# One decoder layer on one core: the first block of x on another queue, a shorter run-up, the first weight cast split over two engines, and one output block of the last 128 tokens in two pieces

## The chip, the cores and the metric

The kernel runs on one core of a Trainium2 chip. The core has TensorE (matmul, written PE in the profile, its weight loads PEld), VectorE (DVE), ScalarE (ACT), GpSimd (POOL) and SyncE (SP); SP and ACT each issue DMAs into a queue of their own (SPq, ACTq). The metric is the device time of one execution in microseconds (us), the median of several runs.

## What is computed

One layer over 256 tokens of width 2048, all in float32:

```
h = rmsnorm(x, norm_mix_w);  proj = h @ w_in          # w_in: 2048 x 16416
q, k, v (conv + silu) -> gated delta rule over 16 heads -> rmsnorm * silu(z)
p_in -> causal means over 2, 4, 8, 16 tokens -> pool_w
x = x + (sigmoid(g_a) * y_a + sigmoid(g_b) * y_b) @ w_out
h = rmsnorm(x, norm_ffn_w);  gate, up = h @ w_up      # 2048 x 11264
x = x + (gelu(conv(gate) + b) * up) @ w_down          # 5632 x 2048
y = rmsnorm(x, norm_final_w)
```

The weights are read once, about 300 MB, and every product is made of three: each float32 operand is split into a high part, rounded to the float32r type in which TensorE multiplies, and a low part, the remainder; high x high, low x high and high x low are summed.

## The kernel before, in words

**Weights.** `srcs` lists the weight blocks in the order of their use, mostly 256 rows x 512 columns (0.5 MB). `load` (L120) has SP read the next block into one of four `raw` buffers; the first two blocks (`HALVES = 2`) are read in two halves of 128 rows each. `begin` (L136) splits a block: ScalarE casts `raw` to `whi` (L144), then VectorE subtracts to get `wlo` (L152). For the first two blocks `begin_half` (L128) does the same for one half at a time (L133, L134).

**Start.** GpSimd writes a tile of ones, and TensorE multiplies ones by ones (`runup`, L241), nine times before anything else; a float32 matmul appears as two records in the profile. The rows of `norm_mix_w` are read by ScalarE's queue (L255); a copy of one column behind that read (L258) has ScalarE load its table early. SP reads x in column blocks of 512, both groups of 128 tokens at once, the first block in two halves of 256 columns (L263). Its row of issues is: x 0 first half, weight block 0 (two halves), x 0 second half, weight block 1 (two halves), x 1, weight blocks 2 and 3, x 2, x 3.

**First products.** From L319 the order of TensorE, VectorE and ScalarE is the order of the program text. TensorE transposes `nmrows` (L321), VectorE copies that to `nmw`. Then, for each of four groups of 128 rows of w_in: TensorE transposes x (`turn_x`, L281; two groups at a time), ScalarE scales the transposed x to its high part `xhi` (L287), VectorE makes the low part `xlo` (L288), `begin_half` splits the half weight block, and TensorE multiplies (`products_k0`, L313): high x high, low x high, high x low, for two groups of tokens each, so six matmuls. Behind the first split stands a second run-up of four matmuls (L332); the products of a group are issued one group later than its split. From the third weight block on, whole blocks are split by `begin`.

**Middle.** All later projections, the delta rule, the pooling, w_out, w_up and w_down follow; TensorE's work there is not touched by the change. Outside L319 to L351 and one later stretch, a planner orders the instructions by a simulated timeline.

**End.** w_down's last products are ordered so that the four column blocks of the first 128 tokens (t = 0) finish ahead of those of the last 128 (t = 1). For each block VectorE adds the residual (L1142), ScalarE sums the squares (L1145), and for blocks 0 to 2 VectorE multiplies by the final gain (L1147). When all blocks of a t are done, the root is taken (L1149 to L1152, the last on GpSimd), and `scaled` multiplies the blocks by it and writes them out: blocks 2 and 3 on VectorE, 0 and 1 on ScalarE, each 128 x 512 with one DMA of 256 KB (L1128), in the order 2, 0, 3 on SP's queue and 1 on ScalarE's.

Of the kernel before, what the change touches and what calls it, by code (L numbers as in the profile page):

```python
# [7 lines left out]
F32 = mybir.dt.float32  # L8
F32R = mybir.dt.float32r
I32 = mybir.dt.int32  # L10
AF = mybir.ActivationFunctionType
ALU = mybir.AluOpType

P = 128
# [20 lines left out]
def kernel(  # L35
# [20 lines left out]
    nc = tc.nc  # L56
# [11 lines left out]
    def nm(s):  # L68
        cnt[0] += 1
        return f"{s}_{cnt[0]}"  # L70

    def pg(shape=(P, 512)):
        return psg.tile(list(shape), F32, tag="g", name=nm("psg"))
# [35 lines left out]
    loads = []  # L109
# [4 lines left out]
    def weights(ahead=AHEAD):  # L114

        begin(taken[0] + ahead + 1)
        taken[0] += 1
        return made[taken[0] - 1]

    def load(n):  # L120
        while len(loads) < min(len(srcs), n):
            src = srcs[len(loads)]
            raw = wpool.tile(list(src.shape), F32, tag="raw", name=nm("raw"), bufs=4)
            for k in range(2) if len(loads) < HALVES else (slice(None),):
                last_load[0] = nc.sync.dma_start(raw[:, k], src[:, k]).ins
            loads.append(raw)

    def begin_half(n, k):  # L128

        if k == 0:  # L130
            made.append(tuple(wpool.tile([P, 2, 512], F32R, tag=tag, name=nm(tag)) for tag in ("whi", "wlo")))
        hi, lo = made[n]
        nc.scalar.copy(hi[:, k], loads[n][:, k])  # L133
        nc.vector.tensor_tensor(lo[:, k], loads[n][:, k], hi[:, k].bitcast(F32), op=ALU.subtract)  # L134

    def begin(n):  # L136
# [104 lines left out]
    def runup(n):  # L241
        for _ in range(n):
            mm(pr0[:, 0, :P], ones, ones, start=True, stop=True)  # L243


    runup(9)

    def mtile(i, shape, dt, name):
        return big.tile(shape, dt, tag=f"m{i}", name=name)

    mix = tc.tile_pool(name="mix", bufs=1)
    mp = mix.__enter__()

    nmrows = mp.tile([KD, P], F32, tag="w1", name="nmrows")
    rows = nc.scalar.dma_start(nmrows, norm_mix_w[0].rearrange("(r p) -> r p", p=P))  # L255
    first = cpool.tile([P, 1], F32, name="first")
    with tc.issue_after(rows.ins):
        nc.scalar.copy(first, ones[:, 0:1])  # L258
    x0 = []
    for c in range(4):  # L260
        xc = mtile(c, [P, 2, 512], F32, f"x0_{c}")
        for h in ((0, 256), (256, 512)) if c == 0 else ((0, 512),):
            nc.sync.dma_start(xc[:, :, h[0] : h[1]], x[0, :, c * 512 + h[0] : c * 512 + h[1]]  # L263
                              .rearrange("(t p) d -> p t d", p=P))
            if h[0] == 0:
                load(min(c + 1, 4))
        x0.append(xc)
        load(min(2 * c + 2, 4))


    nmw = cpool.tile([P, KD], F32, name="nmw")
# [3 lines left out]
    def turn_x(c, ks=range(4)):  # L275

        pts = []
        for k in (4 * c + k for k in ks):
            pt = pg([P, S])
            for t in range(2):  # L280
                nc.tensor.transpose(pt[:, t * P : (t + 1) * P], x0[c][:, t, (k % 4) * P : (k % 4 + 1) * P], ident)  # L281
            pts.append((k, pt))
        return pts

    def parts_x(pts):
        for k, pt in pts:
            hi = nc.scalar.activation(xhi[:, k, :], pt, AF.Copy, scale=nmw[:, k : k + 1])  # L287
            lo = nc.vector.scalar_tensor_tensor(xlo[:, k, :], pt, nmw[:, k : k + 1], xhi[:, k, :].bitcast(F32),  # L288
                                                op0=ALU.mult, op1=ALU.subtract)
        return hi.ins, lo.ins  # L290
# [17 lines left out]
    def products_k0(c, kks, hi, lo):  # L308
        for w, part in ((hi, xh), (hi, xl), (lo, xh)):
            for kk in kks:  # L310
                k = 2 * c + kk
                for t in range(2):
                    mm(ps_k0[:, t, :], part(k, t), w[:, kk, :], start=(k == 0 and w is hi and part is xh),  # L313
                       stop=(k == KD - 1 and w is lo))

    def tile_k0(c):
        products_k0(c, range(2), *weights(-1))

    with tc.manual_schedule(engines={mybir.EngineType.PE, mybir.EngineType.DVE, mybir.EngineType.Activation}):  # L319
        pt = pg()  # L320
        nc.tensor.transpose(pt[:, :KD], nmrows, ident[:KD, :KD])  # L321
        nc.vector.tensor_copy(nmw, pt[:, :KD])

        n = 0
        for c in range(HALVES):
            for k in range(2):
                if k == 0:
                    pts = turn_x(0, (2 * c, 2 * c + 1))
                parts_x(pts[k : k + 1])
                begin_half(c, k)  # L330
                if n == 0:
                    runup(4)  # L332
                else:
                    products_k0((n - 1) // 2, ((n - 1) % 2,), *made[(n - 1) // 2])
                n += 1
        taken[0] = HALVES
        for c in range(4):
            if c:
                tile_k0(2 * c)
            if c < 3:  # L340
                pts = turn_x(c + 1)
                parts_x(pts[:2])
                begin(2 * c + 3)
                last_act, last_dve = parts_x(pts[2:])
                begin(2 * c + 4)
                square_x(c)
            if c:
                tile_k0(2 * c + 1)
            else:
                products_k0(1, (1,), *made[1])  # L350
        square_x(3)  # L351
# [110 lines left out]
    for c in range(2):  # L462
        hi, lo = weights()
        for kk in range(8):
            k = 8 * c + kk
# [399 lines left out]
    for g in range(4):  # L865
# [70 lines left out]
        def gate(ps, tag):  # L936
            th = mp.tile([P, 2, 512], F32, tag=tag, name=nm("gate"))
            for t in range(2):
# [6 lines left out]
                                       op0=ALU.add, op1=ALU.mult)  # L945
# [69 lines left out]
    xt = fp.tile([P, 2, D], F32, name="xt")  # L1015
    for c in range(4):
        cs = slice(c * 512, (c + 1) * 512)
# [4 lines left out]
    for c in range(4):  # L1022
# [4 lines left out]
        xs = xt[:, :, c * 512 : (c + 1) * 512]  # L1027
# [4 lines left out]
        for k2 in range(2):  # L1032
            pt = pg([P, 2, S])
            for kk in range(2):
                k = 4 * c + 2 * k2 + kk
                for t in range(2):
                    nc.tensor.transpose(pt[:, kk, t * P : (t + 1) * P], xt[:, t, k * P : (k + 1) * P], ident)
            for kk in range(2):
                k = 4 * c + 2 * k2 + kk
# [3 lines left out]
                                               op0=ALU.mult, op1=ALU.subtract)  # L1043
# [36 lines left out]
    nfin = big.tile([P, D], F32, tag="xhl", name="nfin")  # L1080
# [34 lines left out]
    rs = cpool.tile([P, 2], F32, name="rsf")  # L1115
    for t in range(2):
        ts = slice(t, t + 1)

        def scaled(c, by, queue):
            xs = xt[:, t, c * 512 : (c + 1) * 512]  # L1120
            if by is nc.scalar:
                nc.scalar.activation(xs, xs, AF.Copy, scale=rs[:, ts])
            elif c < 3:
                nc.vector.tensor_scalar(xs, xs, rs[:, ts], None, op0=ALU.mult)
            else:
                nc.vector.scalar_tensor_tensor(xs, xs, rs[:, ts], nfin[:, c * 512 : (c + 1) * 512],
                                               op0=ALU.mult, op1=ALU.mult)
            queue.dma_start(out[0, t * P : (t + 1) * P, c * 512 : (c + 1) * 512], xs)  # L1128

        blocks = [(c, slice(0, 512), None) for c in range(4 - t)]
        if t:
            blocks += [(3, slice(0, 256), None), (3, slice(256, 512), acc[0][0])]
        for n, (c, cs, ps) in enumerate(blocks):
            more = {} if ps is None else dict(ps=ps, first=2 * (LAST - 1))
            if c:
                down_part(LAST - 1, c, t, *ws[c], cs, **more)
            down_part(LAST, c, t, *wk[c], cs, **more)
            xs = xt[:, t, c * 512 : (c + 1) * 512]  # L1140
            sums = cs if ps is not None else slice(0, 512)
            nc.vector.scalar_tensor_tensor(xs[:, sums], (acc[c][t] if ps is None else ps)[:, sums], rs2[:, ts],  # L1142
                                           xs[:, sums], op0=ALU.mult, op1=ALU.add)
            jk = cpool.tile([P, 512], F32, tag="sqj", name=nm("sqj"))
            nc.scalar.activation(jk[:, cs], xs[:, cs], AF.Square, accum_out=ssq5[:, t, n : n + 1])  # L1145
            if c < 3:
                nc.vector.tensor_tensor(xs, xs, nfin[:, c * 512 : (c + 1) * 512], op=ALU.mult)  # L1147
        n = len(blocks) - 1
        nc.vector.tensor_reduce(part[:, ts], ssq5[:, t, 0:n], axis=mybir.AxisListType.X, op=ALU.add)  # L1149
        nc.vector.tensor_scalar(part[:, ts], part[:, ts], 1.0 / D, EPS, op0=ALU.mult, op1=ALU.add)  # L1150
        nc.vector.tensor_scalar(rs[:, ts], ssq5[:, t, n : n + 1], 1.0 / D, part[:, ts], op0=ALU.mult, op1=ALU.add)
        nc.gpsimd.tensor_tensor(rs[:, ts], rs[:, ts], epsx[:, 0:1], op=ALU.pow)  # L1152
        scaled(2, nc.vector, nc.sync)
        scaled(0, nc.scalar, nc.sync)
        scaled(3, nc.vector, nc.sync)
        scaled(1, nc.scalar, nc.scalar)

# [30 lines left out]
```

## Time and profile before

| | |
|---|---|
| median of 3 runs | 1562.16 us (1561.58 to 1562.27) |
| profiled execution | 1561.54 us, span 1559.8 us |
| mean granted TensorE clock | 0.998 |
| HBM read, written | 297.56 MB, 5.27 MB (194 GB/s over the span) |
| DMA share in the 40 slices | 0.6 to 0.8 in most, 0.2 in the last |

The span runs from the first to the last instruction. In the views, a line of the timeline gives start, length, engine, line of the code, operation, output<-inputs, shapes, and in square brackets the idle time ahead of it with what ended it; a line of the chain of waits gives start, length and what the chain went through; a line of the windows view gives for each engine its busy time and number of instructions, then granted clock, share of the DMA engines and GB/s.

### The profile page before, as it was taken

To read this page: it belongs to the slowest core of one execution; us is meant where nothing else is said; L and a number is where in the kernel's file an instruction comes from. 1 tells how busy PE (TensorE), PEld (TensorE's weight loads), DVE (VectorE), ACT (ScalarE), POOL (GpSimd) and SP (SyncE) were. 2 spreads that over 40 slices of the span, in tenths; PEclk is the share of its full clock that TensorE was granted. 3 is DMA by queue.
4 is the path that set the end of the run, shared out by engine and by line. 5 is a ranking of instruction groups with operands and counts; after the bars stand their busy time and mean duration, and the time that the engine had idled before them with its cause. 6 is when DMAs were issued, how large, how long until landed. Compare 5 with 4: busy or idle time off the path is not lost.

```text
span 1559.8 us, 21250 instructions
## 1 busy us (share of the span) xinstructions
PE 1551.1 (99%) x7996; PEld 1304.0 (84%) x7996; DVE 1092.2 (70%) x1705; ACT 749.2 (48%) x969; POOL 52.2 (3%) x54
## 2 busy tenths in 40 slices
PE   9999999999999999999999999999999999999998
PEld 8878888888888888888888888888888888888886
DVE  6899758996699858896656666776666667444445
ACT  6545445454555445454544544444444444334443
POOL 1020001000010001000000000000000000000000
PEclk9999999999999999999999999999999999999999
DMA  8677657676676656675666666666666666666662
GB/s 273 201 239 200 186 161 223 204 204 183 174 218 202 194 174 191 211 205 174 216 188 176 190 188 189 189 190 188 189 183 195 188 187 212 196 192 210 200 222 93
DMA packets 168229, 304.21 MB, mean 195 GB/s; under 512 B 19235, under 2 KB 22835, under 8 KB 167999
## 3 DMA queue, kind: packets, MB, share of 16 engines
q1 hardware_dynamic: 165104, 297.84, 64.5%
q10 hardware_dynamic: 3022, 5.03, 1.0%
q8 instruction: 62, 1.02, 0.3%
q14 instruction: 41, 0.33, 0.1%
HBM read 297.56 MB, written 5.27 MB: 194 GB/s over the span
## 4 chain that ended last, share of the span: by engine, by line
PE 99%; issue 1%; ACT 0%; DVE 0%; POOL 0%; POOLq 0%
PE psm L182 15%; PE psm L184 15%; PE psm L183 15%; PE psm L206 11%; PE psg L206 10%; PE psg L1094 8%; PE psm L1094 7%; PE psg L207 5%; PE psm L207 5%; PE psm L313 1%; PE psg L672 1%; PE psg L227 1%; PE psg L674 0%; PE psm L243 0%; PE psg L809 0%
## 5 line engine op out<-in xcount | busy, mean ns | idle before, releaser
L152 DVE TENSOR_TENSOR wlo<-raw,whi 128x1024 fp32r<-128x1024 f32 x522 | 636.8, 1222 | 376.6 <-ACT whi L144 372.0
L144 ACT CAST whi<-raw 128x1024 fp32r<-128x1024 f32 x524 | 551.3, 1053 | 699.5 <-PE psm L183 293.8
L184 PE MATMUL psm<-wlo,xhl 128*128 128x512 f32 x864 | 339.1, 393 | 0.0
L183 PE MATMUL psm<-whi,xhl 128*128 128x512 f32 x864 | 339.0, 392 | 0.0
L182 PE MATMUL psm<-whi,xhl 128*128 128x512 f32 x864 | 339.0, 392 | 0.0
L206 PE MATMUL psm<-fhl,whi 128*128 128x512 f32 x704 | 246.2, 396 | 0.0
L206 PE MATMUL psg<-fhl,whi 128*128 128x512 f32 x704 | 238.0, 394 | 0.0
L207 PE MATMUL psm<-fhl,wlo 128*128 128x256 f32 x704 | 194.4, 279 | 0.0
L182 PEld LDWEIGHTS psm<-whi,xhl 128*128 128x128 f32 x864 | 162.3, 188 | 33.0
L183 PEld LDWEIGHTS psm<-whi,xhl 128*128 128x128 f32 x864 | 162.3, 188 | 32.9
L184 PEld LDWEIGHTS psm<-wlo,xhl 128*128 128x128 f32 x864 | 162.2, 188 | 32.7
L207 PE MATMUL psg<-fhl,wlo 128*128 128x256 f32 x704 | 178.7, 279 | 0.0
L206 PEld LDWEIGHTS psm<-fhl,whi 128*128 128x128 f32 x704 | 131.4, 188 | 30.5
L206 PEld LDWEIGHTS psg<-fhl,whi 128*128 128x128 f32 x704 | 129.2, 188 | 24.1
L207 PEld LDWEIGHTS psg<-fhl,wlo 128*128 128x128 f32 x704 | 132.5, 188 | 6.9
L207 PEld LDWEIGHTS psm<-fhl,wlo 128*128 128x128 f32 x704 | 132.6, 188 | 1.1
L1094 PE MATMUL psg<-whi,hhi 128*128 128x512 f32 (+1 forms) x170 | 66.0, 389 | 0.0
L1094 PE MATMUL psg<-whi,hlo 128*128 128x512 f32 (+1 forms) x170 | 65.9, 388 | 0.0
L1094 PE MATMUL psm<-whi,hlo 128*128 128x512 f32 x168 | 65.1, 388 | 0.0
L1094 PE MATMUL psm<-wlo,hhi 128*128 128x512 f32 x168 | 65.1, 388 | 0.0
L1094 PE MATMUL psm<-whi,hhi 128*128 128x512 f32 x168 | 65.1, 388 | 0.0
L1094 PE MATMUL psg<-wlo,hhi 128*128 128x512 f32 (+1 forms) x170 | 59.6, 388 | 0.0
(280 smaller groups left out, 1533.9 us busy)
## 6 DMA issues: line engine op xcount, KB each, us to landing
raw<-in_w_in_dram SPq DMA_DIRECT2D x224, 512.0 KB, 4.3
raw<-in_w_up_dram SPq DMA_DIRECT2D x176, 512.0 KB, 4.4
raw<-in_w_down_dram SPq DMA_DIRECT2D x88, 512.0 KB, 4.3
raw<-in_w_out_dram SPq DMA_DIRECT2D x32, 512.0 KB, 3.8
mv<-vrow SPq DMA_DIRECT2D x12, 512.0 KB, 5.7
taps<-in_conv_qkv_w_dram SPq DMA_DIRECT2D x16, 256.0 KB, 6.0
raw<-in_pool_w_dram SPq DMA_DIRECT2D x8, 512.0 KB, 3.7
vrow<-ev SPq DMA_DIRECT2D x4, 512.0 KB, 4.1
```

Of the source, the lines that this page charges most:

```text
L144: nc.scalar.copy(hi, raw)
L152: last_split[0] = nc.vector.tensor_tensor(lo, raw, hi.bitcast(F32), op=ALU.subtract).ins
L182: mm(ps[:, t, :], lh(k, t), hi[:, kk, :], start=(k == 0), stop=False)
L183: mm(ps[:, t, :], ll(k, t), hi[:, kk, :], start=False, stop=False)
L184: mm(ps[:, t, :], lh(k, t), lo[:, kk, :], start=False, stop=(k == nk - 1))
L206: mm(ps[f], hi[:, kk, fs], rhl(k), start=(k == 0), stop=False, skip_group_check=True)
L207: mm(ps[f][:, 1, :], lo[:, kk, fs], rhl(k)[:, 0, :], start=False, stop=(k == nk - 1), skip_group_check=True)
L227: nc.tensor.transpose(pt[:, ff, t * P : (t + 1) * P], src[:, t, f * P : (f + 1) * P], ident)
L313: mm(ps_k0[:, t, :], part(k, t), w[:, kk, :], start=(k == 0 and w is hi and part is xh), stop=(k == KD - 1 and w is lo))
L672: mm(pg0, kq[:, h, 0, 0:P], kq[:, h, :, :], start=True, stop=True)
L1094: mm(ps[:, cs], part(k, t), w[:, kk, cs], start=(k == first and n == 0), stop=(k == KF - 1 and n == 2), skip_group_check=last_block)
```

## The change

Four edits at the start, one at the end:

- In `begin_half`, the cast of the very first half block is divided: ScalarE casts columns 0 to 255, VectorE columns 256 to 511. The other three half blocks stay as they were.
- `runup(9)` becomes `runup(7)`, and the second run-up `runup(4)` is removed.
- The first half of x's block 0 is read by ScalarE's queue, ahead of `nmrows`.
- SP's row of issues now begins with weight block 0; the rest of it keeps its order.
- `scaled` takes a list of pieces. For t = 1, block 2 is scaled and written in two pieces of 256 columns, so SP issues four writes there instead of three; for t = 0 nothing changes.

```diff
--- before.py
+++ after.py
@@ -130,7 +130,11 @@
         if k == 0:
             made.append(tuple(wpool.tile([P, 2, 512], F32R, tag=tag, name=nm(tag)) for tag in ("whi", "wlo")))
         hi, lo = made[n]
-        nc.scalar.copy(hi[:, k], loads[n][:, k])
+        if n or k:
+            nc.scalar.copy(hi[:, k], loads[n][:, k])
+        else:
+            nc.scalar.copy(hi[:, k, :256], loads[n][:, k, :256])
+            nc.vector.tensor_copy(hi[:, k, 256:], loads[n][:, k, 256:])
         nc.vector.tensor_tensor(lo[:, k], loads[n][:, k], hi[:, k].bitcast(F32), op=ALU.subtract)
 
     def begin(n):
@@ -243,7 +247,7 @@
             mm(pr0[:, 0, :P], ones, ones, start=True, stop=True)
 
 
-    runup(9)
+    runup(7)
 
     def mtile(i, shape, dt, name):
         return big.tile(shape, dt, tag=f"m{i}", name=name)
@@ -251,21 +255,22 @@
     mix = tc.tile_pool(name="mix", bufs=1)
     mp = mix.__enter__()
 
+
+    x0 = [mtile(c, [P, 2, 512], F32, f"x0_{c}") for c in range(4)]
+
+    def load_x(queue, c, h):
+        queue.dma_start(x0[c][:, :, h[0] : h[1]], x[0, :, c * 512 + h[0] : c * 512 + h[1]]
+                        .rearrange("(t p) d -> p t d", p=P))
+
+    load_x(nc.scalar, 0, (0, 256))
     nmrows = mp.tile([KD, P], F32, tag="w1", name="nmrows")
     rows = nc.scalar.dma_start(nmrows, norm_mix_w[0].rearrange("(r p) -> r p", p=P))
     first = cpool.tile([P, 1], F32, name="first")
     with tc.issue_after(rows.ins):
         nc.scalar.copy(first, ones[:, 0:1])
-    x0 = []
-    for c in range(4):
-        xc = mtile(c, [P, 2, 512], F32, f"x0_{c}")
-        for h in ((0, 256), (256, 512)) if c == 0 else ((0, 512),):
-            nc.sync.dma_start(xc[:, :, h[0] : h[1]], x[0, :, c * 512 + h[0] : c * 512 + h[1]]
-                              .rearrange("(t p) d -> p t d", p=P))
-            if h[0] == 0:
-                load(min(c + 1, 4))
-        x0.append(xc)
-        load(min(2 * c + 2, 4))
+    for n, c, h in ((1, 0, (256, 512)), (2, 1, (0, 512)), (4, 2, (0, 512)), (4, 3, (0, 512))):
+        load(n)
+        load_x(nc.sync, c, h)
 
 
     nmw = cpool.tile([P, KD], F32, name="nmw")
@@ -328,9 +333,7 @@
                     pts = turn_x(0, (2 * c, 2 * c + 1))
                 parts_x(pts[k : k + 1])
                 begin_half(c, k)
-                if n == 0:
-                    runup(4)
-                else:
+                if n:
                     products_k0((n - 1) // 2, ((n - 1) % 2,), *made[(n - 1) // 2])
                 n += 1
         taken[0] = HALVES
@@ -1116,16 +1119,17 @@
     for t in range(2):
         ts = slice(t, t + 1)
 
-        def scaled(c, by, queue):
-            xs = xt[:, t, c * 512 : (c + 1) * 512]
-            if by is nc.scalar:
-                nc.scalar.activation(xs, xs, AF.Copy, scale=rs[:, ts])
-            elif c < 3:
-                nc.vector.tensor_scalar(xs, xs, rs[:, ts], None, op0=ALU.mult)
-            else:
-                nc.vector.scalar_tensor_tensor(xs, xs, rs[:, ts], nfin[:, c * 512 : (c + 1) * 512],
-                                               op0=ALU.mult, op1=ALU.mult)
-            queue.dma_start(out[0, t * P : (t + 1) * P, c * 512 : (c + 1) * 512], xs)
+        def scaled(c, by, queue, blocks=((0, 512),)):
+            for begin, end in blocks:
+                cs = slice(c * 512 + begin, c * 512 + end)
+                xs = xt[:, t, cs]
+                if by is nc.scalar:
+                    nc.scalar.activation(xs, xs, AF.Copy, scale=rs[:, ts])
+                elif c < 3:
+                    nc.vector.tensor_scalar(xs, xs, rs[:, ts], None, op0=ALU.mult)
+                else:
+                    nc.vector.scalar_tensor_tensor(xs, xs, rs[:, ts], nfin[:, cs], op0=ALU.mult, op1=ALU.mult)
+                queue.dma_start(out[0, t * P : (t + 1) * P, cs], xs)
 
 
 
@@ -1150,7 +1154,7 @@
         nc.vector.tensor_scalar(part[:, ts], part[:, ts], 1.0 / D, EPS, op0=ALU.mult, op1=ALU.add)
         nc.vector.tensor_scalar(rs[:, ts], ssq5[:, t, n : n + 1], 1.0 / D, part[:, ts], op0=ALU.mult, op1=ALU.add)
         nc.gpsimd.tensor_tensor(rs[:, ts], rs[:, ts], epsx[:, 0:1], op=ALU.pow)
-        scaled(2, nc.vector, nc.sync)
+        scaled(2, nc.vector, nc.sync, ((0, 256), (256, 512)) if t else ((0, 512),))
         scaled(0, nc.scalar, nc.sync)
         scaled(3, nc.vector, nc.sync)
         scaled(1, nc.scalar, nc.scalar)
```

## The prediction

> **What bounds the kernel.** The page first: engine totals and the chain of work that ended last.
>
> ```profile
> span 1559.8 us, 21250 instructions
> ...
> PE 1551.1 (99%) x7996; PEld 1304.0 (84%) x7996; DVE 1092.2 (70%) x1705; ACT 749.2 (48%) x969; POOL 52.2 (3%) x54
> ...
> PE 99%; issue 1%; ACT 0%; DVE 0%; POOL 0%; POOLq 0%
> ```
>
> TensorE is the chain from end to end. What it lacks of the span, 1559.8 - 1551.1 = 8.7 us, is the 1.06 us before its first instruction and about 7.6 us after its last. A change that touches only the two ends can shift the start of the useful matmuls or shorten the time behind the last one; what lies between is carried along. So I read the two ends. The same chain in order of time (start, length, what), its first pieces:
>
> ```profile
> 1.06 4.21 PE psm L243 x18
> ...
> 5.43 0.59 PE psg L281 x4
> 6.01 0.89 PE psm L243 x8
> 6.91 1.61 PE psm L313 x6
> ...
> 8.96 2.76 PE psm L313 x12
> ```
>
> L243 is the run-up: matmuls on ones, two records each. runup(9) gives 18, runup(4) gives 8. The useful products are L313, 2.76 / 12 = 0.23 us each, and everything later follows the first of them. The timeline of all engines there (start, length, engine, line):
>
> ```profile
> 0.80 0.45 ACTq L255 DMA_DIRECT2D nmrows<-in_norm_mix_w_dram  x1
> 0.81 0.43 SPq L263 DMA_DIRECT2D x<-in_x_dram  x1
> ...
> 1.06 3.91 PEld L243 LDWEIGHTS psm<-ones 128*128 128x128 f32 x18 [1.06 <-POOL ones L233]
> ...
> 1.28 0.93 SPq L125 DMA_DIRECT2D raw<-in_w_in_dram  x2
> 1.29 1.28 ACT L258 ACT_TABLE_LOAD   x1 [1.29 <-PEq L1172]
> ...
> 5.19 0.13 PEld L321 LDWEIGHTS psg<-ident,nmrows 16*128 16x128 f32 x1 [0.23 <-issue]
> ...
> 5.83 0.47 ACT L287 ACTIVATE xhl<-psg,nmw 128x256 fp32r<-128x256 f32 x1 [3.05 <-PE psg L281]
> ...
> 6.21 0.61 ACT L133 CAST whi<-raw 128x512 fp32r<-128x512 f32 x1
> 6.34 0.48 DVE L288 SCALAR_TENSOR_TENSOR xhl<-psg,nmw,xhl 128x256 fp32r<-128x256 f32 x1 [0.70 <-ACT xhl L287]
> ...
> 6.85 0.69 DVE L134 TENSOR_TENSOR wlo<-raw,whi 128x512 fp32r<-128x512 f32 x1
> ...
> 6.87 1.20 PE L313 MATMUL psm<-whi,xhl 128*128 128x512 f32 x4
> ```
>
> The issues of the DMAs in the stretch 1.2 to 1.7 us (last column: us from issue to landing):
>
> ```profile
> x<-in_x_dram SPq DMA_DIRECT2D x1, 256.0 KB, 3.2
> raw<-in_w_in_dram SPq DMA_DIRECT2D x1, 256.0 KB, 4.9
> ```
>
> So x's first half block landed at 0.81 + 3.2 = 4.0 and waited until the run-up had left TensorE at 5.19: the run-up, not x, sets the first transpose. The first half of the weights landed at 1.28 + 4.9 = 6.18, and ScalarE cast it at 6.21, as soon as it was there and its own xhi was done. The cast ended at 6.82, the first product began at 6.87. Two chains meet there almost level: run-up, transposes, xhi on one side, the landing of the weights and their cast on the other. Both have to become earlier for a gain.
>
> **The change, part by part: the head.** The run-up loses 2 of its 9 matmuls, four records. Weight loads are spaced (3.91 - 0.33) / 17 = 0.21 us (0.33 is one cold load, an estimate that leaves 17 equal steps), so TensorE is free at about 1.06 + 13 x 0.21 + 0.33 = 4.1 instead of 4.97, and the x that landed at 4.0 would be met.
>
> x by ScalarE's queue: issued at 0.80, as before. What moves is SP's row behind it: the two weight halves start at 0.81 instead of 1.28 and all later loads of the head come 0.47 earlier. Landing of the first weight half: 5.71 if it takes its 4.9 again; bounds 6.18 (nothing gained, the engines are shared) and 4.0 (as fast as x was). I take 5.71. Landing of x: at best 4.0 again, at worst with the weights, 5.7. How much room the DMA engines had (the DMA share and GB/s are the last two columns):
>
> ```profile
> 1.85:3.85 2.00, 2.00 (x12) 2.00 (x11) 1.75 (x7) 0.92 (x2) 1.85 (x5) 1.00 0.81 177
> 3.85:5.85 2.00, 2.00 (x12) 1.75 (x12) 0.17 (x1) 0.02 (x1) 0.03 (x1) 1.00 0.79 246
> 5.85:7.85 2.00, 2.00 (x14) 1.72 (x13) 1.49 (x3) 1.85 (x4) 0.00 (x0) 1.00 1.04 376
> ```
>
> While x moved, 177 GB/s flowed, half of the 376 that the same engines reach 4 us later. There is room for both, so I put x nearer the early end: 4.3. The Trainium skill, DMA: Bandwidth & Descriptors, section "Issuing engines are not separate DMA queues", speaks against the move: both queues run on the same 16 engines and interleave, and a second issuer saves only its issue time. By it x and the weights would land together; that is the first rival.
>
> nmrows, now second in ScalarE's queue, is issued 0.45 later, and so are the table load (to 3.0) and its copy. ScalarE's first real work is at 5.1 or later, so the table is covered. nmrows is 8 KB behind x on the same queue and is needed by the transpose just ahead of x's; without that cover it would cost the 0.45.
>
> From x to the first product: before, 5.83 - 5.19 = 0.64 us from the first transpose to xhi's start. The clock is still slow at 4.3, so I add 0.2 (two transposes at 0.21 in place of 0.11): xhi starts at 5.15. xhi 0.47, then xlo on VectorE, 0.04 after it, 0.48: done at 6.14.
>
> The shared cast: ScalarE takes 256 columns, VectorE the other 256. ScalarE's half: the rows have no cast of that size, but these:
>
> ```profile
> 1551.58 0.42 ACT L1145 ACTIVATE sqj<-xt 128x256 f32<-128x256 f32 x1 [0.71 <-DVE xt L1142]
> ...
> 1554.21 0.49 DVE L1124 TENSOR_SCALAR xt<-xt,rsf 128x512 f32<-128x512 f32 x1 [0.67 <-POOL rsf L1152]
> ```
>
> About 0.4, ending at 5.74 + 0.4 = 6.14 instead of the 0.61 of the whole. VectorE's half is a new instruction behind xlo: between 0.24 (half of L1124's 0.49) and 0.48 (L288, same width); I take 0.36, near the middle, less 0.09 by which such instructions overlap: done at 6.41. The product needs both halves, so the first is at 6.46 instead of 6.87: **-0.4 us**. The cast alone would lose: on the x side it puts xhi-to-product at 0.51 + 0.39 + 0.36 + 0.05 = 1.3 us instead of 6.87 - 5.83 = 1.04. It pays only where the weights land last. wlo, behind the copy, takes 0.69 and ends 0.7 after the first product; its own product is the fifth, 4 x 0.23 = 0.9 us on, so it stays hidden.
>
> Dropping runup(4): its 0.89 us lay between the transposes and the ready cast, so in place it cost nothing, and removing it gives nothing by itself; it would be in the way once the cast is ready earlier. In its stead TensorE idles about 1 us.
>
> What comes next must keep up. The next weight block:
>
> ```profile
> raw<-in_w_in_dram SPq DMA_DIRECT2D x1, 256.0 KB, 5.5
> ...
> 2.73 0.94 SPq L125 DMA_DIRECT2D raw<-in_w_in_dram  x2
> ...
> 9.15 0.61 ACT L133 CAST whi<-raw 128x512 fp32r<-128x512 f32 x1
> ...
> 13.80 1.68 PEld L313 LDWEIGHTS psm<-whi,xhl 128*128 128x128 f32 x8 [0.26 <-ACT whi L144]
> ```
>
> It landed at 2.73 + 5.5 = 8.2 and was cast at 9.15: 0.9 us to spare, and its issue moves 0.47 forward with the rest. The 0.26 at 13.80 is TensorE waiting for a cast that waits for its own transposes; it moves along. So the 0.4 survives.
>
> **The tail.** Of the last 128 tokens, block 2 is scaled and written in two pieces.
>
> ```profile
> 1554.20 1.33 ACT L1122 ACTIVATE xt<-xt,rsf 128x512 f32<-128x512 f32 x2 [0.92 <-POOL rsf L1152]
> ...
> 1554.61 0.75 DVE L1126 SCALAR_TENSOR_TENSOR xt<-xt,rsf,nfin 128x512 f32<-128x512 f32 x1
> 1554.72 1.30 SPq L1128 DMA_DIRECT2D out_dram<-xt  x3
> 1555.57 0.37 ACTq L1128 DMA_DIRECT2D out_dram<-xt  x1
> ...
> 1555.50:1558.30 2.80, 0.00 (x0) 0.00 (x0) 0.00 (x0) 0.04 (x1) 0.00 (x0) 0.50 1.00 369
> ...
> DMA packets 137, 0.20 MB, mean 340 GB/s; under 512 B 14, under 2 KB 61, under 8 KB 137
> ```
>
> From 1555.5 to 1558.3 the DMA engines are full (share 1.00): the four writes, 1.05 MB, end when the bytes are through, so the start of the first write counts. Its piece of 256 columns is ready after 0.24 to 0.49, say 0.35: issued at 1554.58 instead of 1554.72, -0.14. SP then has four issues instead of three, 1.30 / 3 = 0.43 each; the last begins near 1555.9 instead of 1555.6, still ahead of the bytes queued before it. VectorE's block 3 ends about 0.15 later than before, hidden behind SP's row. Pieces have 1 KB rows instead of 2 KB: in the head's stretch 5.0 to 5.6, with 61 - 14 = 47 of 123 data packets that small, 340 GB/s instead of 369 flowed, 8% less; all small, some 20% on 0.26 MB, 0.14 us. So the tail is about -0.05 with bounds -0.25 (earlier start, no price) and +0.4 (a whole SP issue on the end).
>
> **Sum.** -0.4 - 0.05 = -0.45 us. The profiled execution took 1561.54 (span 1559.8 and 1.7 around it), 0.6 under the median 1562.16 of three runs; I put the same step on both: 1561.1 by the profile, **1561.7** by the median, which I forecast.
>
> **Rivals.**
> A, slower: x shares the DMA engines with the first weights and lands with them, 0.80 + 4.9 = 5.7. Then xhi starts at 5.7 + 0.64 = 6.34 and the first product, 1.3 on, at 7.64: +0.75, 1562.9. It decides from where x lands after 4.95 (xhi at 5.59, product at 6.87). For it: 177 GB/s may be all that the first microseconds give; against it: the engines were 0.81 busy, not full.
> B, nothing gained at the landing: the weights still come at 6.18, since the same bytes are ahead of them. ScalarE's half ends at 6.6, the product begins at 6.65: -0.2, with the tail 1561.9.
> C, the clock. The run-up's 0.21 us a step against 0.89 / 8 = 0.11 in the second run-up shows TensorE's slow stretch: from 1.06 to at least 4.97, 3.9 us, though the granted clock reads 1.00 there. After the change TensorE does nothing for about 1 us before the first product, and may wait for x before that. If the warming has to begin again with the products, 3.9 us run at 0.11 / 0.21 of the pace: 3.9 x (1 - 0.52) = +1.9, in all +1.4, 1563.6. Against it: up to the idle TensorE has been at work for some 4 us, as long as before. The Trainium skill, TensorE: Matmul & The Clock Gate, "Part 1: The HAM clock gate", says the clock is set by a free-running window of about 3.4 us; by that a missed window costs 3.4 us at half pace, about +1.7, and it differs from run to run. No row here shows the window.
>
> **How the numbers follow.** The forecast 45%, A 20%, B 15%, C 15%, and 5% for the planner laying out the later work differently, either way. The early ends together (weights and x at 4.0, copy 0.24) give a first product near 6.0: -0.9 and the tail -0.25, so 1561.0 on the median; the profile lies 0.6 under the median, so single sessions differ by as much: low 1560.6. C sets the high end, 1563.6. A measurement of this kernel tells about 0.2%, 3.1 us, from no change. No case reaches it: faster needs more than the whole head up to the first product could give, slower needs A and C together with more. Same 0.91, faster 0.03, slower 0.06 for what the planner may do.
>
> **What would show it.** Right: run-up of 14 records ending near 4.1, x landed by 4.3, first L313 near 6.45, steps of 0.23 from there; first output issue near 1554.6 less the head's shift. A: the x landing at 5 or later and xhi behind it. B: weights landing at 6.2. C: L313 steps of 0.4 or more. The forecast falls if the first L313 is not earlier than 6.87, or if TensorE waits anew between 7 and 15 us.

## The result, and the profile after

| | before | after |
|---|---|---|
| median (8 runs each) | 1562.04 us (1561.32 to 1563.05) | 1566.55 us (1566.19 to 1567.11) |
| ratio after to before | | 1.003, interval 1.002 to 1.004 |
| profiled execution, span | 1561.54 us, 1559.8 us | 1566.50 us, 1564.8 us |
| mean granted clock | 0.998 | 0.998 |

The change made the kernel slower by 4.5 us, 0.3%; the forecast was 1561.7. The timeline of after at the start (start, length, engine, line, tile, and in brackets the idle time ahead with what ended it); the run-up is now L247, the nmrows transpose L326, x's transposes L286, the products L318:

```profile
0.80 0.48 ACTq L262 DMA_DIRECT2D x<-in_x_dram  x1
0.80 0.85 SPq L125 DMA_DIRECT2D raw<-in_w_in_dram  x2
1.06 3.06 PEld L247 LDWEIGHTS psm<-ones 128*128 128x128 f32 x14 [1.06 <-POOL ones L237]
1.31 0.48 ACTq L267 DMA_DIRECT2D nmrows<-in_norm_mix_w_dram  x1
...
6.87 0.26 PE L326 MATMUL psg<-ident,nmrows 16*128 16x16 f32 x1 [2.46 <-DMA nmrows<-in_norm_mix_w_dram]
7.05 0.72 PEld L286 LDWEIGHTS psg<-ident,x 128*128 128x128 f32 x4
...
7.78 0.47 ACT L292 ACTIVATE xhl<-psg,nmw 128x256 fp32r<-128x256 f32 x1 [4.47 <-PE psg L286]
8.15 0.40 ACT L136 CAST whi<-raw 128x256 fp32r<-128x256 f32 x1
...
8.69 0.28 DVE L137 CAST whi<-raw 128x256 fp32r<-128x256 f32 x1
...
9.12 2.04 PE L318 MATMUL psm<-whi,xhl 128*128 128x512 f32 x4 [0.95 <-DVE whi L137]
10.96 1.05 PE L318 MATMUL psm<-wlo,xhl 128*128 128x512 f32 x2
...
17.60 1.67 PEld L318 LDWEIGHTS psm<-whi,xhl 128*128 128x128 f32 x8 [0.26 <-ACT whi L148]
```

The run-up's weight loads end at 1.06 + 3.06 = 4.1, as worked out. Then TensorE waits 2.46 us for 8 KB: nmrows, issued at 1.31 behind x, arrives at 6.7. The first product starts at 9.12 instead of 6.87. It is also slow: four records take 2.04 us where before they took 1.20, and the weight loads of x's four transposes 0.72 instead of 0.42, though the granted clock reads 1.00 up to 12 us. (The trace's record of the clock begins with its first rise, at 5.20 before and only at 12.51 after; the views put 1.00 where there is no record.) From 13.80 before, 17.60 after, the same weight load has the same length again, 3.80 us later.

Where the weights went ahead of x, the DMA view of after shows: all packets between 1.8 and 2.8 us, by queue (packets, MB, share of the 16 engines; q1 is SP's queue, q10 ScalarE's), then the same second of before.

```profile
DMA packets 67, 0.14 MB, mean 137 GB/s; under 512 B 0, under 2 KB 0, under 8 KB 67
...
q1 hardware_dynamic: 67, 0.14, 94.5%
```

```profile
DMA packets 211, 0.19 MB, mean 194 GB/s; under 512 B 19, under 2 KB 207, under 8 KB 211
...
q1 hardware_dynamic: 183, 0.19, 62.9%
q10 hardware_dynamic: 28, 0.01, 3.2%
```

Before, x (1 KB packets) led SP's row and nmrows' few packets went through beside it. After, x and the weights were issued at the same moment, 0.80, and for a whole microsecond only the weights' 2 KB packets moved, at 137 GB/s; not one packet of ScalarE's queue, so neither x nor the nmrows behind it. From then on both queues move side by side; the same view of after, 2.8 to 5.2 us:

```profile
q10 hardware_dynamic: 271, 0.26, 47.1%
q1 hardware_dynamic: 122, 0.21, 38.3%
```

These 0.26 MB on q10 are x's 256 KB. By the packets in the trace, x moved from 2.86 to 5.24, before from 1.88 to 3.73. By the semaphore updates that end a read, x landed at 5.60, before at 4.05, and nmrows, whose packets follow x's, at 6.73. Of the 1.55 us that x lands later, 0.98 is the later first packet and the rest is the sharing. x alone would have held the first transpose up by 0.4 us, from 5.19 to 5.60; the rest of the 1.65 in the table below is nmrows.

From 13.8 us the shift between the two profiles stays 3.80 to 490 us. Then it grows twice, each time where a read of data that the kernel wrote to DRAM itself lands later. The tile lb near 490 us, before and after (DVE waiting for it; then the time from issue to landing of its four reads):

```profile
487.30 0.42 DVE L736 TENSOR_TENSOR tmp<-lb,tb 128x248 f32<-128x248 f32 x1 [0.68 <-DMA lb<-cdd]
...
lb<-cdd SPq DMA_DIRECT2D x4, 128.0 KB, 5.1
...
TT<-tbd SPq DMA_DIRECT2D x4, 32.0 KB, 1.8
```

```profile
493.22 0.42 DVE L739 TENSOR_TENSOR tmp<-lb,tb 128x248 f32<-128x248 f32 x1 [2.81 <-DMA lb<-cdd]
...
lb<-cdd SPq DMA_DIRECT2D x4, 128.0 KB, 7.9
...
TT<-tbd SPq DMA_DIRECT2D x4, 32.0 KB, 3.1
```

VectorE waits 2.81 us instead of 0.68, its wlo (the low part of a weight block) comes late, and TensorE loses 0.63 us between 490 and 502. TT, near 717 us, lands 3.1 us after its issue instead of 1.8 and costs another 0.30. At the end (timeline, then one stretch of the windows view, whose last three columns are clock, DMA share and GB/s):

```profile
1558.93 1.34 ACT L1127 ACTIVATE xt<-xt,rsf 128x512 f32<-128x512 f32 x2 [0.91 <-POOL rsf L1156]
1558.93 0.62 DVE L1129 TENSOR_SCALAR xt<-xt,rsf 128x256 f32<-128x256 f32 x2 [0.67 <-POOL rsf L1156]
1559.31 1.80 SPq L1132 DMA_DIRECT2D out_dram<-xt  x4
...
1560.30 0.35 ACTq L1132 DMA_DIRECT2D out_dram<-xt  x1
```

```profile
1560.00:1563.20 3.20, 0.00 (x0) 0.00 (x0) 0.21 (x1) 0.27 (x1) 0.00 (x0) 0.50 0.89 326
```

The scaling starts 1558.93 - 1554.20 = 4.73 later than before, and the span is 5.0 longer, so the tail itself took 0.27 more. Added up, by the start of the same instruction in both profiles:

| up to | shift so far | what was added |
|---|---|---|
| nmrows transpose (5.19, 6.84) | +1.65 | nmrows lands late, behind a late x |
| first product (6.87, 9.12) | +2.25 | 0.30 transposes at the slow clock, 0.30 shared cast |
| load at 13.80, 17.60 | +3.80 | 1.55, products at the slow clock |
| 502 us | +4.43 | 0.63, lb |
| scaling (1554.20, 1558.93) | +4.73 | 0.30, TT |
| end of the span | +5.0 | 0.27, tail |

### The profile page after: what moved, and what is told of

Read it like the earlier page. It is cut to its first block, busy times and chain, and to the rows that moved or that the text cites. A ratio compares the mean times of both kernels' runs of the same rounds, so it can differ in the third digit from the quotient of the medians.

```text
span 1564.8 us, 21231 instructions
## 1 busy us (share of the span) xinstructions
PE 1552.3 (99%) x7984; PEld 1303.4 (83%) x7984; DVE 1092.5 (70%) x1707; ACT 748.7 (48%) x969; POOL 52.2 (3%) x54
## 4 chain that ended last, share of the span: by engine, by line
PE 98%; DMA 1%; issue 1%; DVE 0%; ACT 0%; SPq 0%; POOLq 0%; POOL 0%; ACTq 0%; DVEq 0%
PE psm L186 15%; PE psm L188 15%; PE psm L187 15%; PE psm L210 10%; PE psg L210 10%; PE psg L1097 7%; PE psm L1097 7%; PE psg L211 5%; PE psm L211 5%; PE psm L318 2%; PE psg L675 1%; PE psg L231 1%; PE psg L677 0%; DMA nmrows<-in_norm_mix_w_dram 0%; PE psg L820 0%
```

## The experiments

Each was timed in ten runs, and the kernel before beside it on the same chip; ratios are to it, with their interval. Dots in a diff stand for lines of it that are not shown. The first four ask which part of the head costs the time.

**Only the move** (kernel before, first half of x on ScalarE's queue, SP's row beginning with the weights; run-ups, cast and tail as before):

```diff
+    load_x(nc.scalar, 0, (0, 256))
     nmrows = mp.tile([KD, P], F32, tag="w1", name="nmrows")
...
-        for h in ((0, 256), (256, 512)) if c == 0 else ((0, 512),):
-            nc.sync.dma_start(...)
...
+    for n, c, h in ((1, 0, (256, 512)), (2, 1, (0, 512)), (4, 2, (0, 512)), (4, 3, (0, 512))):
+        load(n)
+        load_x(nc.sync, c, h)
```

> The kernel before with one edit: the first half block of x goes to ScalarE's queue ahead of nmrows, and SP's row begins with the weights; run-up, cast and tail as before. Theory (the move makes x and nmrows land late, and the shorter run-up then leaves the clock slow): nmrows lands near 6.7 us again and the first transpose is near 6.8 instead of 5.19; the clock has turned by 5 us under the long run-up, so the first product is near 6.87 + 1.65 = 8.5 and later steps are 0.23; in all +1.6 us. Rival (the run-up alone is at fault, the move costs nothing): within 0.3 us of before.

1564.32 against 1561.94, ratio 1.0014 (1.0004 to 1.0023). TensorE in its timeline:

```profile
6.68 0.25 PE L321 MATMUL psg<-ident,nmrows 16*128 16x16 f32 x1 [1.42 <-DMA nmrows<-in_norm_mix_w_dram]
6.86 1.11 PE L281 MATMUL psg<-ident,x 128*128 128x128 f32 x4
7.77 1.91 PE L243 MATMUL psm<-ones 128*128 128x128 f32 x8
9.34 1.42 PE L313 MATMUL psm<-whi,xhl 128*128 128x512 f32 x4
```

The move alone brings the wait for nmrows. It brings the slow clock too, in spite of the long run-up: the second run-up takes 1.91 for the 8 records that took 0.89 before, and in the 1.42 us ahead TensorE had stood still. The shift is 2.47 at the first product, where 1.65 was expected, 2.8 once the clock is up, and has no step at 490 us.

**x back** (the changed kernel with x at the head of SP's row again):

```diff
-    load_x(nc.scalar, 0, (0, 256))
     nmrows = mp.tile([KD, P], F32, tag="w1", name="nmrows")
...
-    for n, c, h in ((1, 0, (256, 512)), (2, 1, (0, 512)), (4, 2, (0, 512)), (4, 3, (0, 512))):
-        load(n)
-        load_x(nc.sync, c, h)
+        for h in ((0, 256), (256, 512)) if c == 0 else ((0, 512),):
+            nc.sync.dma_start(...)
...
```

> The changed kernel with x back at the head of SP's row, nmrows first on ScalarE's queue; short run-up, shared cast and split tail kept. Theory: transposes start near 4.2 us, first product near 6.6, and the products run at 0.23 us a step as TensorE was at work up to 5 us; in all -0.3 to +0.3 us, the tail's +0.27 included. Rival (the run-up is at fault): products at 0.43 us a step until about 10 us, in all +1.2 us or more.

1563.78, ratio 1.0006 (0.9997 to 1.0016), and the runs fall into two groups: four at 1562.1 to 1562.6, six at 1563.8 to 1564.7. The profiled run is of the lower group:

```profile
4.56 0.83 PE L285 MATMUL psg<-ident,x 128*128 128x128 f32 x4
6.84 1.20 PE L317 MATMUL psm<-whi,xhl 128*128 128x512 f32 x4 [1.44 <-ACT whi L136]
```

Here the transposes are early, as the prediction wanted them, but the product is at 6.84 against 6.87: the weights land at 1.28 + 5.1 = 6.38, 0.2 later than before, and the time won is spent in waiting for them. From their landing to the product it is 0.46 us, before 6.87 - 6.18 = 0.69: where the weights land last, the shared cast does gain. In the six profiles with this row of issues (before, x back, cast and tail, short run-up, keep warm, few wide) the first half of the weights took 4.5 to 5.2 us, a spread larger than the 0.4 us that the change was to gain. At 490 us 0.43 is added, at the tail 0.25. The upper group of runs has no profile here.

**nmrows first** (the changed kernel, nmrows ahead of x on ScalarE's queue):

```diff
-    load_x(nc.scalar, 0, (0, 256))
     nmrows = mp.tile([KD, P], F32, tag="w1", name="nmrows")
     rows = nc.scalar.dma_start(nmrows, norm_mix_w[0].rearrange("(r p) -> r p", p=P))
+    load_x(nc.scalar, 0, (0, 256))
```

> The changed kernel with the two reads on ScalarE's queue in the other order: nmrows, then x. Theory (x itself is late, as its packets share the DMA engines with the first weights): the nmrows transpose moves to about 4.2 us, but the first x transpose waits for x until 5.5 to 6.2; clock still slow; in all +2.5 to +4 us. Rival (only the small nmrows read, stuck behind x, was late): x transposes near 4.3, first product near 6.5, in all -0.4 to +1 us.

1566.08, ratio 1.0025 (1.0016 to 1.0035). The wait moves from nmrows to x:

```profile
4.34 0.28 PE L326 MATMUL psg<-ident,nmrows 16*128 16x16 f32 x1
6.53 1.11 PE L286 MATMUL psg<-ident,x 128*128 128x128 f32 x4 [1.90 <-DMA x<-in_x_dram]
8.59 2.04 PE L318 MATMUL psm<-whi,xhl 128*128 128x512 f32 x4 [0.95 <-DVE whi L137]
```

nmrows is there at 4.3, x, issued 0.45 us later than in the changed kernel, only at 6.5. So the small load alone was not the fault: whichever of the two stands second on ScalarE's queue is late, and x was late at its head too (5.60).

**Long run-up** (the changed kernel with 16 matmuls ahead, so that TensorE works until nmrows is there):

```diff
-    runup(7)
+    runup(16)
```

> The changed kernel with 16 matmuls of run-up in place of 7, so that TensorE is at work until about the time nmrows lands (6.7 us). Theory: first transpose near 6.8 as in the changed kernel, but transposes and products at full pace (0.11 and 0.23 us a step): the 1.5 us lost between the first product and 12.5 us and 0.3 before it come back, in all +2.2 to +2.8 us against before instead of +4.5. Rival (the slow steps come from contention with the DMAs or from the casts, not from the clock): steps stay at 0.43, in all +4 us or more.

1564.17, ratio 1.0013 (1.0003 to 1.0022).

```profile
1.06 6.46 PE L247 MATMUL psm<-ones 128*128 128x128 f32 x32 [1.06 <-POOL ones L237]
7.45 0.23 PE L326 MATMUL psg<-ident,nmrows 16*128 16x16 f32 x1
...
9.43 1.16 PE L318 MATMUL psm<-whi,xhl 128*128 128x512 f32 x4 [1.16 <-DVE whi L137]
```

The run-up outlasts nmrows by 0.6 us, the first product is 0.31 later than in the changed kernel, and yet the distance to the kernel before falls from 4.5 to 2.2 us: the products run at full pace from the first. The shift is 2.52 and stays there; the step at 490 us is gone as well.

**Cast and tail** (kernel before with only the shared cast and the divided last write):

```diff
+        if n or k:
+            nc.scalar.copy(hi[:, k], loads[n][:, k])
+        else:
+            nc.scalar.copy(hi[:, k, :256], loads[n][:, k, :256])
+            nc.vector.tensor_copy(hi[:, k, 256:], loads[n][:, k, 256:])
...
+        scaled(2, nc.vector, nc.sync, ((0, 256), (256, 512)) if t else ((0, 512),))
```

> The kernel before with the shared first cast and the split last block alone; run-up and the order of reads as before. Theory: VectorE's copy stands behind xlo, so the first product comes 0.2 to 0.3 us later than 6.87; the tail from the root on GpSimd to the end is 0.25 us longer (4 issues in SP's row and rows of 1 KB); the clock is not touched. In all +0.4 to +0.6 us by the profile. Rival (both edits gain, as the prediction had it for the tail): tail -0.05, in all within 0.25 us.

1562.38, ratio 1.0003 (0.9994 to 1.0012). In its timeline:

```profile
6.13 0.47 ACT L291 ACTIVATE xhl<-psg,nmw 128x256 fp32r<-128x256 f32 x1 [3.36 <-PE psg L285]
...
7.04 0.28 DVE L137 CAST whi<-raw 128x256 fp32r<-128x256 f32 x1
...
7.47 1.16 PE L317 MATMUL psm<-whi,xhl 128*128 128x512 f32 x4
```

From xhi's start to the product 1.34 us, where before it was 1.04: VectorE takes its half only behind xlo. The tail is 0.25 longer. (The other 0.30 at 6.13 against 5.83 is the slow clock, in the transposes of this one execution, whose clock first rises at 6.55.) So in this profile both parts cost a quarter of a microsecond each; the medians, 0.4 apart, agree, but their interval holds no change too. The profile also loses another 0.35 us near 681 us; the cause is open.

**Short run-up only** (kernel before with 7 matmuls ahead and none behind):

```diff
-    runup(9)
+    runup(7)
...
-                if n == 0:
-                    runup(4)
-                else:
+                if n:
```

> The kernel before with the short run-up alone: 7 matmuls, and none behind the first split. Theory: x has landed at 4.0, the transposes start near 4.35, but the first product stays at 6.87, as the weights land at 6.18; TensorE idles some 1.5 us. Whether the clock has turned by then differs from run to run: part of the runs as before, part about 1.5 to 2 us longer, like the x_back kernel's 1562.1 to 1562.6 and 1563.8 to 1564.6. Rival (the second group of those runs came from the cast or the tail): all runs within 0.7 us of before's median.

1562.95, ratio 1.0007 (0.9998 to 1.0017), again two groups: five runs at 1561.9 to 1562.6, five at 1563.3 to 1565.6. The profiled run, 1564.05, is of the upper group. TensorE in the windows view (busy time, granted clock, DMA share, GB/s):

```profile
5.20:6.60 1.40, 0.00 (x0) 1.00 1.01 345
6.60:7.60 1.00, 0.99 (x4) 0.99 0.98 354
7.60:9.20 1.60, 1.60 (x7) 0.50 1.00 321
9.20:11.00 1.80, 1.80 (x6) 0.50 1.05 405
```

The first four records run at full pace, then the granted clock drops to 0.50, behind an idle stretch of only 1.5 us. Its first product is at 6.61, 0.26 earlier than before, as the weights landed at 5.9; then 1.6 us are lost by 11 us, about the distance of the two groups. Some 0.7 more is added at 490 us, and 0.45 near 681, where the cause is open.

**Head start** (the changed kernel with nmrows at the head of SP's row: x alone on ScalarE's queue, the weights issued 0.4 us behind it; the copy that has ScalarE load its table now waits for x's issue):

```diff
-    rows = nc.scalar.dma_start(nmrows, norm_mix_w[0].rearrange("(r p) -> r p", p=P))
+    nc.sync.dma_start(nmrows, norm_mix_w[0].rearrange("(r p) -> r p", p=P))
...
```

> The changed kernel with nmrows moved from ScalarE's queue to the head of SP's row: x is still read by ScalarE's queue, but now alone and with the weights issued some 0.4 us behind it. Theory (x was late because the first weights' packets came ahead of its own on the same DMA engines): x lands at 4.0 to 4.5 as it did on SP's queue, weights near 6.2, first product near 6.8; in all 0 to +2 us, by the clock. Rival (ScalarE's queue itself is slow to start): x lands after 5, the first x transpose is at 5.3 or later and the runs are +3 us or more.

1562.79, ratio 1.0005 (0.9996 to 1.0014); five runs at 1561.3 to 1562.2, five at 1563.4 to 1564.3. The DMA view up to 2.8 us, and TensorE's timeline:

```profile
q10 hardware_dynamic: 205, 0.21, 31.2%
q1 hardware_dynamic: 34, 0.01, 7.3%
```

```profile
4.56 1.11 PE L286 MATMUL psg<-ident,x 128*128 128x128 f32 x4
6.62 2.05 PE L318 MATMUL psm<-whi,xhl 128*128 128x512 f32 x4 [0.95 <-DVE whi L137]
```

Now x's packets move first, it is there at 4.56 without a wait, and the weights still land at 5.98. So ScalarE's queue is not slower than SP's: which row gets its packets out first decides. With this one line the product is at 6.62, 0.25 ahead of before. Slow steps take that back in the profiled run, one of the upper group, and the step at 490 us and the longer tail come on top.

**Keep warm** (kernel before with 7 matmuls ahead, 6 in place of 4 behind the first split, and the shared cast):

```diff
...
-    runup(9)
+    runup(7)
...
-                    runup(4)
+                    runup(6)
```

> The kernel before with the run-up divided otherwise: 7 matmuls ahead of the transposes and 6 behind the first split, and with the shared first cast; reads and tail as before. Theory: transposes near 4.3, TensorE at work until the product is ready, so the clock turns as in the kernel before; first product 6.7 to 6.9, in all -0.2 to +0.1 us, and no second group of runs 1.5 us up. Rival (the idle stretch does not matter, the shorter first run-up does): a second group as in the x_back kernel.

1562.02, ratio 1.0002 (0.9992 to 1.0011), all ten runs between 1561.3 and 1562.7. With the same start of the run-up as in the short one but no idle stretch behind it, the upper group is gone. The product is at 7.18 here, though x landed at 4.8 and both halves of the cast were done by 6.76:

```profile
5.52 1.72 PEld L247 LDWEIGHTS psm<-ones 128*128 128x128 f32 x12
...
6.46 0.28 DVE L137 CAST whi<-raw 128x256 fp32r<-128x256 f32 x1
```

The second run-up's loads hold TensorE until 5.52 + 1.72 = 7.24, so nothing is won either. A filling that ends with the cast was not tried.

**Few, wide run-up matmuls** (kernel before with 4 matmuls over 512 columns ahead and 3 small ones behind: 7 instructions in place of 13, TensorE busy throughout; `runup` gets an argument `wide` for it). It separates the step at 490 us, so far seen in just the kernels with 7 run-up matmuls, from the clock:

```diff
...
-    runup(9)
+    runup(4, wide=True)
...
-                    runup(4)
+                    runup(3)
```

> The kernel before with the run-up made of 7 instructions instead of 13, but as long: four matmuls over 512 columns ahead of the transposes, three over 128 behind the first split. Reads, cast and tail as before. Theory (the step near 490 us belongs to the number of TensorE's instructions: a 16 KB fetch of its instructions comes 4 us later against the code and falls into the four reads of lb, which then land after 8 us instead of 5.1): first product within 0.2 us of before, full pace, the step of 0.4 to 0.7 us between 490 and 502 us there; in all +0.3 to +0.7 us. Rival (the step comes from the slow clock or from the shift of the start): no step, in all within 0.2 us.

1564.01, ratio 1.0013 (1.0004 to 1.0023). The run-up lasted 1.57 us longer than meant, until 6.7, and the shift is 1.6 from there to 490 us at full pace throughout. Then it grows by 0.75:

```profile
491.08 0.42 DVE L739 TENSOR_TENSOR tmp<-lb,tb 128x248 f32<-128x248 f32 x1 [2.88 <-DMA lb<-cdd]
```

```profile
q8 instruction: 1, 0.02, 0.7%
...
lb<-cdd SPq DMA_DIRECT2D x4, 128.0 KB, 8.2
```

The step is there with a warm clock, so the clock is not its cause. Nor is the shift of the start: move only (2.8) and long run-up (2.5) have a shift and no step, x back a step and no shift. The number of instructions ahead is what the kernels with the step share. What goes with it: program code arrives in fetches of 16 KB, and one falls among lb's reads (the q8 row; after has it too, before has none in this stretch). Over before, after and the nine kernels, lb landed in 5.1 to 5.5 us in the five whose fetch came before lb's issue, and in 7.9 to 8.3 in the six whose fetch came during its reads; these six are those with 7 run-up matmuls. That one fetch of about 1 us on one engine can hold four reads back by 3 us is read from this pattern, and not shown by itself.

The pattern returns at other reads of this kind. Near 717 us a fetch falls among TT's reads in after; from the DMA view of after, 717.1 to 720.0:

```profile
q8 instruction: 1, 0.02, 2.1%
```

The six kernels with 7 run-up matmuls all have a fetch there, and TT landed in 2.3 to 3.1 us; in the other five it falls elsewhere, and TT landed in 1.8 to 1.9. An earlier TT, near 362, shows the same (3.2 to 3.8 against 1.6 to 1.7). For an earlier lb, near 123, it is the other way round: there the fetch falls among the reads of the other five, and they are the late ones (5.1 to 6.2 against 4.0 to 4.5). Near 660, where no kernel has a fetch, lb landed in 4.3 to 4.7 in all eleven. Near 182 and 302 the picture is mixed.

## Why the prediction was wrong, by its steps

**The landing of x, and of nmrows behind it, is the step that failed**: "There is room for both, so I put x nearer the early end: 4.3." x landed at 5.60, near the late end of 5.7. The 177 GB/s were read as half-used engines, but the same line has the engines 0.81 busy: a fifth was free, not half. In the first microsecond of traffic (1.8 to 2.8) the weights alone, issued at the same moment, held 94.5% of the engines at 137 GB/s; x's packets began a microsecond later than before and then shared the engines. The rule of the Trainium skill (DMA: Bandwidth & Descriptors, "Issuing engines are not separate DMA queues") was on the right side, and rival A with it, but both queues "interleave" by that page, and here they did so only from 2.8 us on: the weights came at 0.80 + 4.1 = 4.9, earlier than the 5.71 taken, x 0.7 later.

**nmrows** was said to be covered by x, or to cost 0.45 without the cover. It landed 1.1 us behind the late x and set the path at 6.7: with x's own part 1.65.

**The clock.** Rival C had its price nearly right (+1.9; measured 0.30 + 1.55), and its chance and its place wrong. The clock did not fall and begin anew: in the changed kernel it had not risen at all before 12.51. A and C were kept apart as exclusive, when A's wait is what makes TensorE idle and so causes C: in the kernels with the wait (move only, nmrows first and the changed one) no profiled run was without a slow stretch. Added, A's +0.75 and C's +1.9 would have given 1564.8. The second run-up was priced at nothing since it lay in a gap; its work was to fill that gap. With keep warm, the short first run-up has one group of runs, without a second run-up two. The text had it that a slowdown beyond 3.1 us needs A and C together with more, and gave that no chance: its 0.06 was the planner's.

**The shared cast** went as worked out: 1.34 for the 1.3 of the sum, VectorE's copy 0.28 for 0.36. As the prediction says, it pays only where the weights land last, and here they landed first; it cost 0.30.

**The tail.** The first write did start earlier behind the scaling, 1559.31 - 1558.93 = 0.38 for 0.52, the predicted -0.14. The sum of -0.05 was mis-sized (its own two terms, -0.14 and +0.14, come to nothing): SP's four issues take 1.80 us, 0.45 each, so the last one begins 1.4 after the first instead of 0.9, and the engines, full before (share 1.00, 369 GB/s), stand at 0.89 and 326. Measured +0.27, inside the bound of +0.4.

**What was not in the prediction** is the 0.63 at 490 and the 0.30 at 717 us. "What lies between is carried along" holds for TensorE's own work; reads by DMA that end just in time do not move as a block with it. Both go with a fetch of program code among the reads, which six matmuls fewer had moved there.

Right were the end of the run-up (4.1), the start of the issues, the weights landing earlier, and that the order of the later work stayed.

Left open: why of two loads issued at the same moment the weights' packets went first, why these move at 137 GB/s only (no run tried either), and how a fetch of code would hold the reads up. No version was faster than the kernel before: the earliest first products, 6.61 with the short run-up and 6.62 with the head start, are 0.25 ahead, and their lower groups of runs lie within the runs of before.

## What to carry to other kernels

Two loads issued at the same moment on two queues are not two half-speed loads: at the start of this kernel one moved its first packet a microsecond after the other and then shared the engines with it. So the load on the critical path needs to be issued first, whatever the queue, and a small one that is needed with it should not stand behind it (head start has it on the other queue). Filler work on the bounding engine is priced by what its clock does without it, not by the gap that it fills. Where one mechanism's wait is another's condition, their prices add and their chances do not exclude each other.

## What the runs showed of the hardware

**A short idle stretch can be enough to halve the clock.** 1.5 us without work (short run-up, 5.1 to 6.6) were followed by 0.50 from 7.6 to 11.0 in the profiled run, and by their times about half of the runs are like it; x back has 1.44 us without work, and its profiled run stayed at full pace. The Trainium skill, TensorE: Matmul & The Clock Gate, "Part 1: The HAM clock gate", speaks of a free-running window of some 3.4 us and of one idle window before the clock falls. Two groups of runs agree with a window that runs on its own, and so do the turns of the short run-up's clock, at 4.17, 7.59 and 11.00, 3.4 us apart; that the idle stretch has to be 3.4 us long does not hold here.

**The clock rose only behind a filled stretch.** In all eleven profiles TensorE was at work for 3.1 us or more of the 3.41 ahead of the first rise (3.39 in the changed kernel, 9.10 to 12.51). The changed kernel's earlier stretches of that length had 2.13 (2.28 to 5.69) and 1.30 (5.69 to 9.10), and no rise came. Its seven matmuls keep TensorE at work for 3.35 us only.

**The granted clock does not show the slow start.** In after it reads 1.00 up to 12.4 us while the products' steps are twice as long (1.05 us for two records, against 0.62 in the long run-up), as the record begins with the first rise; in the short run-up, where the clock had risen before, it reads 0.50. The steps are the surer sign.

**The number of instructions moves the fetches of code, and late reads go with them.** Six TensorE matmuls fewer at the start went with a read near 490 us that landed 3 us later, whether the clock was slow or not, and with one near 123 us that landed earlier.
